# Which projection runs beside which mixer: Hyena's beside HGRN2, Mamba's beside Hyena, attention's beside Mamba

## Chip, cores and metric

One core of a Trainium2 chip. The metric is the device time of one launch, in microseconds (us).

## What is computed

A bidirectional encoder of two layers over a sequence of 512 positions and 1024 channels, all in float32. Each layer projects the normalised input once, lets four mixers work on slices of the projection's columns, projects their results back, and adds a mixture of 16 experts in which each expert chooses its 64 positions:

```
for l in range(DEPTH):
    hn = rmsnorm(x, norm_mix_w[l])
    pa, pb, pc, pd = jnp.split(hn @ w_in[l], splits, axis=-1)
    ya = hyena_mixer(pa, ...)                 # short conv, long conv by FFT, gate
    yb = mamba2_mixer(pb, ...)                # conv of 5 taps, silu, two scans, gate, rmsnorm
    yc = dilated_attention_mixer(pc, rel_bias)
    yd = hgrn2_mixer(pd, ...)                 # gated linear attention, two directions
    x = x + jnp.concatenate([ya, yb, yc, yd], axis=-1) @ w_out[l]
    x = x + expert_choice_moe(rmsnorm(x, norm_ffn_w[l]), router_w[l], ...)
return rmsnorm(x, final_norm_w)
```

The mixers do not depend on one another; only their sum does on all four. Each can thus run at any time once its own slice of the projection is there.

## The kernel before

One program computes everything; activations stay on the chip, weights are streamed in. The code is written as Python generators (`encoder`): each mixer and each projection is a stream that emits some instructions and then yields the weight of what it emitted. `weave` (L428) takes turns between two streams, always the one whose sum of yielded weights, divided by the number given with it, is least, until both are done; `chain` puts streams one after the other. The text order that comes out is the priority; a scheduler then places each engine's instructions in a fixed order, and `slots_in_order` (L157) holds tiles that share the same slots to the order of the text. The rings of slots that matter here are `bank_a`, three PSUM banks for `pcm`, `ptm` and `po`; `S`, three split weights; `W`, two raw weights; and `G`, nine pages for small temporaries.

A layer's mixers are written in four stages (L1590 to L1597). In each, one mixer (`hgrn`, `mamba`, `hyena`, `attn`), whose steps are short and hang on one another, is woven with work that does not depend on it: the projections of a later mixer and parts of the output projection.

The projections do their matmuls in three parts each, on weights and activations split into a high and a low part. `proj_cm` (L395 to L397) gives channels on partitions: 24 matmuls on one PSUM bank (`pcm`). `proj_tm` (L417 to L419) gives positions on partitions: 24 matmuls (`ptm`) for each of four blocks of 128 positions. The weight is split by GpSimd and VectorE (L380, L381), or by ScalarE and VectorE (L377, L378). `mamba_proj` (L685) computes four channel blocks with `proj_cm`, runs conv taps on each (L712 and L713 on VectorE) and a silu of three ScalarE activations (`me`, L446 to L448) and a multiplication (L449), and then one `proj_tm`. `hyena_proj` (L562 on) has six channel blocks, with two taps on each (L577, L578) and no silu. `attn_proj` (L917 on) has queries and keys by `proj_cm` (`aqs`, `aks`) and values by `proj_tm`.

Of the mixers, these lines matter. In `hgrn`, for each of two directions, the keys are transposed and copied by ScalarE (`gkT`, L1137), multiplied into states (`gU`, L1143), scanned on VectorE, the scores `gsc` (L1165) masked into `gP` (L1170, L1171), and both summed into `go` (L1177, L1186). At the end `go` is squared on ScalarE (`gsq`, L1195), normalised and gated on VectorE (`gy`, L1201 to L1203) and transposed by TensorE (`gyT`, L1208). `mamba` ends with `mo` (L860), its sums, gate and norm on VectorE and ScalarE, and the transposes `myT` (L893). `hyena` goes through transforms `hU` (L624), products with the filter's spectrum on VectorE (L629 to L658, the last of them `hz`), and the inverse transform `hy` (L668). `out_proj(l, [3])` adds HGRN2's part of the output projection (`po`, L1228 to L1230; 48 matmuls), and so needs `gyT`.

Behind the mixers come router and experts. Their weights are loaded ahead on SyncE's queue (`pieces`, the `we` loads of L1402), wherever a buffer is free; `atab` (L964), attention's four tables of position biases, are loaded there too, into buffers that the normalised input (`hT`) leaves.

Of the kernel before, what the change touches and what calls it, by code (L numbers as in the profile page):

```python
# [10 lines left out]
F32 = mybir.dt.float32  # L11
# [88 lines left out]
HW, HY = 28, 6  # L100
# [10 lines left out]
def encoder(ctx: ExitStack, tc: tile.TileContext, d, out, dbg=None, stages=None, nlayers=NL):  # L111
# [82 lines left out]
    def show(name, ap):  # L194
        if dbg and name in dbg:
            SY.dma_start(dbg[name], ap)
# [19 lines left out]
    def xrow(t):  # L216
        return X[t]
# [210 lines left out]
    def weave(*streams):  # L428

        at = [0.0] * len(streams)  # L430
        live = set(range(len(streams)))
        while live:
            i = min(live, key=lambda j: at[j] / streams[j][0])
            w = next(streams[i][1], None)
            if w is None:
                live.discard(i)
            else:
                at[i] += w

    def chain(*gens):  # L440
        for g in gens:
            yield from g
# [8 lines left out]
    MIX = {}  # L451
# [129 lines left out]
    def hyena_proj(l, hT, cols, st):  # L581
        raw1 = w_raw(l, HY0 + 256, 256)
        raw2 = w_raw(l, HY0 + 512, 256)
        uT = tl("N", [4, 256], "uT")

        def turn(c, a):
            ps = bank_a("uTp")
            for t in range(4):
                T.transpose(ps[:, t * P:(t + 1) * P], a[:, t::4], ident)
            A.activation(uT[:, :, c * P:(c + 1) * P], ps.rearrange("p (t c) -> p t c", t=4), AF.Copy)  # L590

        m = []
        for c in range(2):
            a = hyena_conv(hT, raw1, c * P, 2 + c, cols, tl("E", [L], "hu"))
            yield 5.1
            b = hyena_conv(hT, raw2, c * P, 4 + c, cols, tl("E", [L], "hu"))
            m.append(page([L], "hm"))
            V.tensor_mul(m[c], a, b)
            yield 5.1
        raw0 = w_raw(l, HY0, 256)  # L600
        x0 = tl("N", [2, L], "hx0")
        for c in range(2):
            hyena_conv(hT, raw0, c * P, c, cols, x0[:, c])
            turn(c, m[c])
            yield 6.0
        st[:] = uT, x0
# [78 lines left out]
    def mamba_proj(l, hT, cols, st):  # L685
        zt = tl("N", [4, 256], "mz")
        pack = tl("B", [576], "mpack")
        wdt = pack[:, 0:64].rearrange("p (k c) -> p k c", k=8)
        SY.dma_start(wdt, d["w_in"][l][:, MD0:MD0 + 8].rearrange("(k p) c -> p k c", p=P))

        def use(t, ps):
            V.tensor_scalar_max(zt[:, t], ps[:, :256], FLOOR)
            V.tensor_copy(pack[:, 64 + 8 * t:72 + 8 * t], ps[:, 256:264])

        xbc = []
        for ct in (2, 3, 0, 1):
            if ct % 2 == 0:
                raw = w_raw(l, MX0 + ct * P, 256)
                ub = tl("N", [2, L], "mu")
            ps = proj_cm(hT, raw, (ct % 2) * P)  # L700
            u = ub[:, ct % 2]

            def w(k):
                i = R_MCW + k * 4 + ct
                return cols[:, i:i + 1]

            A.activation(u, ps, AF.Identity, scale=w(2), bias=cols[:, R_MCB + ct:R_MCB + ct + 1])
            for k in (0, 1, 3, 4):
                s = k - 2
                o = slice(max(0, -s), L - max(0, s))  # L710
                i = slice(max(0, s), L - max(0, -s))
                V.scalar_tensor_tensor(u[:, o], ps[:, i], w(k), u[:, o], op0=ALU.mult, op1=ALU.add)  # L712
            V.tensor_scalar_max(u, u, FLOOR)  # L713
            e = tl("E", [L], "me")
            silu_inplace(u, e, u)
            xbc.append(u)
            yield 5.1
        yield from proj_tm(l, hT, [(MZ0, 256), (MD0, 8)], use, raws=[w_raw(l, MZ0, 256), wdt])
        st[:] = zt, pack, xbc
# [194 lines left out]
    def attn_proj(l, hT, st):  # L914


        half = (slice(0, 64), slice(64, 128))  # L917
        raw = w_raw(l, AQ0, 256)
        QS = []
        for i in range(2):  # L920
            ps = proj_cm(hT, raw, i * P, AM[0])
            qs = tl("N", [2, L], "aqs", F32R)
            for h in range(2):
                a, b = half[h], half[1 - h]
                A.activation(qs[a, h], ps[a], AF.Copy, scale=0.125)
                V.scalar_tensor_tensor(qs[b, h], ps[a], 0.125, qs[a, h].bitcast(F32),  # L926
                                       op0=ALU.mult, op1=ALU.subtract)
            QS.append(qs)
            yield 5.1
        raw = w_raw(l, AQ0 + 256, 256)  # L930
        KS = []
        for i in range(2):
            ps = proj_cm(hT, raw, i * P, AM[1])
            kh, kl = (tl("N", [2, L], "aks", F32R) for _ in range(2))
            for h in range(2):
                a, b = half[h], half[1 - h]
                A.activation(kh[a, h], ps[a], AF.Copy)
                V.tensor_sub(kl[a, h], ps[a], kh[a, h].bitcast(F32))
                if AM[2]:
                    A.activation(kh[b, h], kh[a, h].bitcast(F32), AF.Copy)  # L940
                    A.activation(kl[b, h], kl[a, h].bitcast(F32), AF.Copy)
                else:
                    G.tensor_copy(kh[b, h], kh[a, h])
                    G.tensor_copy(kl[b, h], kl[a, h])
            KS.append((kh, kl))
            yield 5.1
        v = tl("N", [4, 256], "av")

        def use(t, ps):
            A.activation(v[:, t], ps[:, :256], AF.Copy)  # L950

        yield from proj_tm(l, hT, [(AQ0 + 512, 256)], use, AM[3])
        st[:] = QS, KS, v
# [280 lines left out]
    def out_proj(l, ms):  # L1234
        raws = {m: out_raw(l, m) for m in ms}
        for n in range(2):
            W = {m: out_halves(raws[m], n) for m in ms}
            for t in range(4):
                out_part(t, n, [(m, k) for m in ms for k in range(2)], W)
                yield 1.28 * len(ms)  # L1240
# [318 lines left out]
    cols = [None] * NL  # L1559
    mbc = [None] * NL  # L1560
    fc = [None] * NL
    rows = iter(())
    spec = {}
    act_set(LNEXP)
    for l in range(nlayers):
        hT = norm_T(l, rows)
        s_h, s_m, s_y, s_a = [], [], [], []
        if l == 0:
            masks()
            proj = hgrn_proj(l, hT, s_h)  # L1570
            next(proj)
            inputs = filter_inputs()
            cols[0] = param_columns(0)
            for _ in range(FW[0]):
                next(proj)
            filt = filter_hidden(cols[0], spec, *inputs)
            next(filt)
            cols[1] = param_columns(1)
            hm = page([2, P], "hm", I32)
            SY.dma_start(hm, d["c_hmask"])  # L1580
            G.tensor_scalar(hmask, hm, 1, None, op0=ALU.mult)
            lb = lower_bounds(cols[1])
            scr = attn_table()
            for m in range(NL):
                mbc[m] = mamba_consts(m)
                fc[m] = ffn_consts(m)
            weave((FW[2] + 12, filt), (50, proj))
        else:
            run(hgrn_proj(l, hT, s_h))
        weave((40, hgrn(l, s_h, cols[l], lb)), (31, mamba_proj(l, hT, cols[l], s_m)))  # L1590
        show(f"mix3_{l}", MIX[3][0].bitcast(F32))
        weave((35, mamba(l, s_m, mbc[l], cols[l])), (32, hyena_proj(l, hT, cols[l], s_y)))
        show(f"mix1_{l}", MIX[1][0].bitcast(F32))
        weave((HW, hyena(l, s_y, spec)), (41, chain(out_proj(l, [3]), attn_proj(l, hT, s_a))))
        show(f"mix0_{l}", MIX[0][0].bitcast(F32))
        W = {}
        weave((40, attn(l, s_a, scr)), (25, chain(out_proj(l, [1, 0]), out_last(l, 2, W))))  # L1597
        show(f"mix2_{l}", MIX[2][0].bitcast(F32))
        view = {}
        load_next = pieces(l, view)  # L1600
        ring[:] = FIRST + ["H"] * 7 + EARLY
        while ring:
            next(load_next)
        st = []
        xd = dp.tile([2 * L, L], F32, name=f"xd{l}")
        route = router(fc[l][1], st, xd)
        for t in range(4):
            for n in range(2):
                out_part(t, n, [(2, 1)], W[n])
            next(route)  # L1610
        run(route)
        for t in range(4):
            show(f"xm{l}_{t}", xrow(t))
        if "moe" in stages:
            ra, = st
            rows = moe(l, ra, fc[l][0], load_next, view, xd, filter_again(spec) if l + 1 < nlayers else None)
# [32 lines left out]
```

## Time and profile before

| | us |
|---|---|
| median of 3 runs (1626.92 to 1629.75) | 1627.19 |
| the profiled execution | 1630.68 |
| its span | 1628.9 |
| TensorE busy (matmuls) in it | 1499.7 (92%) |
| VectorE | 789.8 (48%) |
| ScalarE | 394.0 (24%) |
| GpSimd | 212.2 (13%) |

The mean granted TensorE clock is 0.976 of full speed. The core moves 468.62 MB by DMA, most of it expert weights. In layer 0 the four mixer stages run from about 94 to 164 (HGRN2), 164 to 229 (Mamba), 229 to 276 (Hyena) and from 276 on (attention); experts start about 366. Layer 1 does the same some 795 us later. PE is TensorE's matmul, PEld its weight load, DVE VectorE, ACT ScalarE, POOL GpSimd, SP SyncE. In a timeline a row is one instruction or several alike, with the idle time before it and what released it in brackets; the name before the arrow is the tile written, those after it the tiles read.

### The profile page before, as it was taken

The numbers are of one execution on the slowest core, as the hardware profiler recorded it, in microseconds if no ns is written. First come the engines' busy times: TensorE is split into PE (matmuls) and PEld (weight loads), VectorE is DVE, ScalarE is ACT, GpSimd is POOL, SyncE is SP. The second block draws the span as 40 slices with busy tenths as digits, with TensorE's granted clock in tenths as the row PEclk, the third lists the DMA queues.
The fourth block names the chain that finished last, engine by engine and source line by source line (L and its number), as shares of the span: only waits on it lengthen the run. The fifth ranks groups of instructions, "written<-read, shape, count | busy, mean of one in ns | idle before, by whom it ended". The sixth has DMA issues, their size and how long they took to land.

```text
span 1628.9 us, 23876 instructions
## 1 busy us (share of the span) xinstructions
PE 1499.7 (92%) x9475; PEld 854.3 (52%) x9475; DVE 789.8 (48%) x1715; ACT 394.0 (24%) x805; POOL 212.2 (13%) x202
## 2 busy tenths in 40 slices
PE   7988999989999997989879899999899999998986
PEld 6677788753433442334368777787334433332332
DVE  6777777562333331432245777856523433332323
ACT  5244424430000000001162444343210101000012
POOL 3233232000000000000032323300000000000001
PEclk9999999989999999999999999999899999999999
DMA  5410225679999999999933211277799999999996
GB/s 172 128 53 28 79 78 185 228 266 367 421 419 421 421 419 400 421 420 419 421 115 104 79 53 53 78 282 267 251 420 421 418 421 421 421 420 420 420 420 255
DMA packets 153778, 468.62 MB, mean 288 GB/s; under 512 B 20440, under 2 KB 56696, under 8 KB 144962
## 3 DMA queue, kind: packets, MB, share of 16 engines
q1 hardware_dynamic: 145030, 455.10, 71.2%
q0 software_dynamic: 2240, 7.34, 1.1%
q10 hardware_dynamic: 6396, 4.65, 0.9%
q8 instruction: 75, 1.23, 0.3%
q14 instruction: 37, 0.30, 0.1%
HBM read 460.60 MB, written 6.44 MB: 287 GB/s over the span
## 4 chain that ended last, share of the span: by engine, by line
PE 59%; DMA 23%; DVE 8%; issue 4%; ACT 3%; POOL 2%; ACTq 0%; SPq 0%; DVEq 0%; POOLq 0%
PE eg L1410 10%; DMA we<-in_moe_w_down_dram 9%; PE ey L1410 8%; PE eu L1410 8%; DMA we<-in_moe_w_up_dram 8%; DMA we<-in_moe_w_gate_dram 5%; PE pcm L397 3%; PE pcm L395 3%; PE pcm L396 3%; PE ec L1481 2%; PE po L1228 2%; PE po L1229 2%; PE po L1230 2%; PE apv L992 1%; PE ptm L418 1%
## 5 line engine op out<-in xcount | busy, mean ns | idle before, releaser
L1410 PE MATMUL eu<-we,exT 128*64 128x512 f32 x1024 | 236.4, 598 | 16.5 <-DMA we<-in_moe_w_up_dram 14.4
L1410 PE MATMUL ey<-we,ehT 128*64 128x512 f32 x1024 | 233.7, 603 | 18.7 <-ACT ehT L1446 11.2
L1410 PE MATMUL eg<-we,exT 128*64 128x512 f32 x1024 | 229.9, 597 | 10.4 <-DMA we<-in_moe_w_gate_dram 6.2
L1410 PEld LDWEIGHTS eu<-we,exT 128*64 128x64 f32 x1024 | 68.4, 137 | 178.8 <-issue 94.4
L1309 DVE SCALAR_TENSOR_TENSOR ra<-er,ra,tie 128x512 bf16<-128x512 f32 x128 | 95.9, 749 | 127.5 <-PE er L1317 124.6
L1410 PEld LDWEIGHTS ey<-we,ehT 128*64 128x64 f32 x1024 | 71.2, 138 | 156.3 <-issue 106.1
L1410 PEld LDWEIGHTS eg<-we,exT 128*64 128x64 f32 x1024 | 69.3, 137 | 149.4 <-issue 112.0
L1463 DVE SCALAR_TENSOR_TENSOR eY<-ey,erg,eY 64x512 fp32r<-64x512 f32 x64 | 48.0, 749 | 191.2 <-ACT eY L1462 191.2
L1431 ACT ACTIVATE eh<-eg 128x512 f32<-128x512 f32 x32 | 19.1, 598 | 496.6 <-PE eg L1410 496.6
L397 PE MATMUL pcm<-hT,whl 128*128 128x512 f32 x320 | 129.3, 404 | 3.5 <-DVE whl L381 3.5
L1354 POOL DMA_INDIRECT exe<-xd,erow x28 | 27.8, 994 | 790.3 <-DVE erg L1335 663.0
L1482 DVE TENSOR_TENSOR x<-x,ec 128x512 f32<-128x512 f32 x128 | 81.0, 691 | 102.7 <-PE ec L1481 102.7
L395 PE MATMUL pcm<-hT,whl 128*128 128x512 f32 x320 | 129.6, 405 | 0.0
L396 PE MATMUL pcm<-hT,whl 128*128 128x512 f32 x320 | 129.4, 404 | 0.0
L1462 ACT ACTIVATE eY<-ey,erg 64x512 fp32r<-64x512 f32 x64 | 43.6, 682 | 269.9 <-PE ey L1410 245.5
L1438 DVE TENSOR_TENSOR eh<-eh,eu 128x512 f32<-128x512 f32 x32 | 22.0, 688 | 151.8 <-PE eu L1410 151.8
L417 PE MATMUL ptm<-wtm,hT 128*128 128x256 f32 (+1 forms) x256 | 76.0, 298 | 1.9 <-DVE aqs L926 1.7
L1481 PE MATMUL ec<-eY,eot 128*128 128x512 f32 x256 | 67.4, 405 | 10.2 <-DVE erow L1352 6.4
L418 PE MATMUL ptm<-wtm,hT 128*128 128x256 f32 (+1 forms) x256 | 74.7, 293 | 1.9 <-DVE wtm L381 1.9
L380 POOL TENSOR_SCALAR whl<-wraw 128x1024 fp32r<-128x1024 f32 x40 | 48.8, 1220 | 195.1 <-PE pcm L397 95.3
L419 PE MATMUL ptm<-wtm,hT 128*128 128x256 f32 (+1 forms) x256 | 73.5, 291 | 0.0
L397 PEld LDWEIGHTS pcm<-hT,whl 128*128 128x128 f32 x320 | 62.2, 194 | 19.0 <-DVE whl L381 3.9
(394 smaller groups left out, 2298.4 us busy)
## 6 DMA issues: line engine op xcount, KB each, us to landing
we<-in_moe_w_gate_dram SPq DMA_DIRECT2D x218, 512.0 KB
we<-in_moe_w_up_dram SPq DMA_DIRECT2D x208, 512.0 KB
we<-in_moe_w_down_dram SPq DMA_DIRECT2D x206, 512.0 KB
wraw<-in_w_in_dram SPq DMA_DIRECT2D x27, 1024.0 KB
we<-in_moe_w_down_dram SPq DMA_DIRECT2D x25, 1024.0 KB
we<-in_moe_w_up_dram SPq DMA_DIRECT2D x24, 1024.0 KB
we<-in_moe_w_gate_dram SPq DMA_DIRECT2D x19, 1024.0 KB
wo<-in_w_out_dram SPq DMA_DIRECT2D x8, 1024.0 KB
```

The source lines that it names most:

```text
L380: G.tensor_scalar(dst_hi, raw, 1.0, 0.0, op0=ALU.mult, op1=ALU.add)
L395: T.matmul(ps, w[:, 0, k, :], H[k], start=(k == 0), stop=False)
L396: T.matmul(ps, w[:, 0, k, :], Lo[k], start=False, stop=False)
L397: T.matmul(ps, w[:, 1, k, :], H[k], start=False, stop=(k == 7))
L417: T.matmul(dst, h, w[:, 0, k % 4], start=(k == 0), stop=False)
L418: T.matmul(dst, h, w[:, 1, k % 4], start=False, stop=False)
L419: T.matmul(dst, g, w[:, 0, k % 4], start=False, stop=(k == 7))
L1309: V.scalar_tensor_tensor(g, pr, ra[:, c, e, 0:1], tie[:, 384 - c * P:896 - c * P], op0=ALU.subtract, op1=ALU.is_gt, accum_out=k)
L1410: T.matmul(ps[f][64 * f:64 * f + 64], xT[:, j, h], qs[4 * h + j][:, f * 512:(f + 1) * 512], start=(h == 0 and j == 0), stop=(h == 1 and j ...
L1463: V.scalar_tensor_tensor(lo, src, w[c, 0:1], hi.bitcast(F32), op0=ALU.mult, op1=ALU.subtract)
L1481: T.matmul(ps, ot[:, t * P:(t + 1) * P], Y[i][q][n], start=(q == 0), stop=(q == 1))
L1482: V.tensor_add(xrow(t)[:, c], xrow(t)[:, c], ps)
```

## The change

Which projection is woven with which mixer. HGRN2's stage gets `hyena_proj` in place of `mamba_proj`; the second stage becomes Hyena's, beside `out_proj(l, [3])` and `mamba_proj`; the third becomes Mamba's, beside `attn_proj`. So Hyena runs ahead of Mamba. The fourth stage (attention) is as it was. The edit stands in the loop over layers, so it holds for both.

```diff
-        weave((40, hgrn(l, s_h, cols[l], lb)), (31, mamba_proj(l, hT, cols[l], s_m)))
+        weave((40, hgrn(l, s_h, cols[l], lb)), (32, hyena_proj(l, hT, cols[l], s_y)))
         show(f"mix3_{l}", MIX[3][0].bitcast(F32))
-        weave((35, mamba(l, s_m, mbc[l], cols[l])), (32, hyena_proj(l, hT, cols[l], s_y)))
+        weave((HW, hyena(l, s_y, spec)), (41, chain(out_proj(l, [3]), mamba_proj(l, hT, cols[l], s_m))))
+        show(f"mix0_{l}", MIX[0][0].bitcast(F32))
+        weave((35, mamba(l, s_m, mbc[l], cols[l])), (31, attn_proj(l, hT, s_a)))
         show(f"mix1_{l}", MIX[1][0].bitcast(F32))
-        weave((HW, hyena(l, s_y, spec)), (41, chain(out_proj(l, [3]), attn_proj(l, hT, s_a))))
-        show(f"mix0_{l}", MIX[0][0].bitcast(F32))
         W = {}
         weave((40, attn(l, s_a, scr)), (25, chain(out_proj(l, [1, 0]), out_last(l, 2, W))))
```

What it moves on TensorE's queue is shown at three places of layer 0. First the end of HGRN2, before. `pcm_1800` and `pcm_1871` are channel blocks of `hyena_proj`, the rows ahead of these are the last `go` and 21 more matmuls of `pcm_1800`:

```order
L395 MATMUL pcm_1800<-hT_124,whl_1797 128x512
L396 MATMUL pcm_1800<-hT_128,whl_1797 128x512
L397 MATMUL pcm_1800<-hT_124,whl_1797 128x512
L395 MATMUL pcm_1871<-hT_121,whl_1868 128x512
L1208 MATMUL gyT_1763<-pk,gy_1741 128x128 x4
L1208 MATMUL gyT_1770<-pk,gy_1741 128x128 x4
L748 MATMUL mcum_1828<-mpack_910,pk 128x4x4 x2
L749 MATMUL mcum_1828<-mpack_910,ones 128x32
```

And with the change, from the last `go` on; `po` is `out_proj(l, [3])`:

```order
L1186 MATMUL go_947<-gR_1401,gqi_1320 32x64
L1186 MATMUL go_947<-gR_1402,gqi_1320 32x64
L1186 MATMUL go_947<-gR_1401,gqi_1320 32x64
L1208 MATMUL gyT_1692<-pk,gy_1670 128x128 x4
L1208 MATMUL gyT_1699<-pk,gy_1670 128x128 x4
L1228 MATMUL po_1729<-wos_1726,mxh_1690 128x512
L1229 MATMUL po_1729<-wos_1726,mxh_1690 128x512
```

The 25 matmuls of `hyena_proj` that stood between `go` and `gyT` are no longer there: `gyT` follows the last `go`, and the output projection follows `gyT`.

Second, the middle of HGRN2: the last scores and the first products `go` of the second direction. Before, with `ptm_1590` and `ptm_1663` of `mamba_proj`:

```order
L419 MATMUL ptm_1663<-wtm_1391,hT_125 128x264
L417 MATMUL ptm_1663<-wtm_1391,hT_122 128x264
L418 MATMUL ptm_1663<-wtm_1391,hT_122 128x264
L1177 MATMUL go_954<-gv_260,gP_1585 32x64 x4
L1177 MATMUL go_955<-gv_260,gP_1585 32x64 x4
```

And with the change, where `uTp_1567` is four transposes of `hyena_proj`'s product:

```order
L1165 MATMUL gsc_1466<-gqk_1318,gqk_1319 32x32
L1165 MATMUL gsc_1465<-gqk_1318,gqk_1319 32x32
L1165 MATMUL gsc_1466<-gqk_1318,gqk_1319 32x32
L589 MATMUL uTp_1567<-pk,hm_1294 128x128 x4
L1177 MATMUL go_946<-gv_260,gP_1531 32x64 x4
L1177 MATMUL go_947<-gv_260,gP_1531 32x64 x4
```

The 22 `ptm` matmuls between the last `gsc` and the first `go` are gone; one group of transposes is there in their place.

Third, the end of Mamba. Before, with `po` of `out_proj(l, [3])`, 44 of which stand between the last `mo` and `myT`:

```order
L1228 MATMUL po_2401<-wos_2382,mxh_1761 128x512
L1229 MATMUL po_2401<-wos_2382,mxh_1761 128x512
L1230 MATMUL po_2401<-wos_2382,mxl_1762 128x512
L1228 MATMUL po_2420<-wos_2382,mxh_1761 128x512
L893 MATMUL myT_2303<-pk,my_1977 128x128
L893 MATMUL myT_2310<-pk,my_1977 128x128
```

And with the change; `ptm_2660` is the last block of `attn_proj`, and `alog` is attention's first product:

```order
L418 MATMUL ptm_2660<-wtm_2512,hT_124 128x256
L419 MATMUL ptm_2660<-wtm_2512,hT_128 128x256
L854 MATMUL my_2686<-mxt_2225,mw_2596 128x64 x4
L860 MATMUL mo_2691<-mprev_2278,mu_1822 128x256
L860 MATMUL mo_2692<-mprev_2278,mu_1822 128x256
L893 MATMUL myT_2728<-pk,my_2362 128x128 x4
L893 MATMUL myT_2735<-pk,my_2362 128x128 x4
L969 MATMUL alog_2749<-aks_2339,aqs_2201 128x512
L969 MATMUL alog_2749<-aks_2340,aqs_2201 128x512
L1228 MATMUL po_2767<-wos_2761,mxh_2726 128x512
```

`myT` follows `mo` directly, and attention and the rest of the output projection stand behind it.

## Rows read from the trace of the kernel before

**Rows 1.** the page's slices: DMA share in 40 equal slices of the span, in tenths

```profile
DMA  5410225679999999999933211277799999999996
```

**Rows 2.** chain of waits in the expert stages, by window: start us, us, what

```profile
567.51 12.85 DMA we<-in_moe_w_down_dram
...
1596.28 12.33 DMA we<-in_moe_w_down_dram
```

**Rows 3.** windows ahead of layer 0's experts: us, PE, PEld, DVE, ACT, POOL, PEclk, DMA share, GB/s

```profile
360.00:370.00 10.00, 9.08 (x54) 3.59 (x54) 5.38 (x19) 1.88 (x2) 0.00 (x0) 0.92 0.22 68
370.00:380.00 10.00, 10.00 (x64) 3.67 (x62) 3.00 (x10) 1.19 (x2) 0.00 (x0) 1.00 0.97 363
```

**Rows 4.** windows over three mixer stages of layer 0, same columns

```profile
94.00:164.00 70.00, 57.30 (x967) 47.60 (x966) 55.38 (x82) 34.17 (x54) 24.96 (x20) 0.90 0.16 47
164.00:229.00 65.00, 63.48 (x376) 50.19 (x375) 49.47 (x110) 27.34 (x74) 18.79 (x17) 1.00 0.25 75
229.00:276.00 47.00, 44.38 (x245) 38.79 (x244) 34.30 (x50) 16.04 (x27) 13.91 (x10) 0.93 0.37 128
```

**Rows 5.** waits of TensorE in layer 0, 86 to 276: total us, times, longest

```profile
PE gU L1143 <- ACT gkT L1137: 9.4, 2, 6.2
PE go L1177 <- DVE gP L1171: 2.3, 1, 2.3
PE pcm L397 <- DVE whl L381: 1.7, 1, 1.7
PE gyT L1208 <- DVE gy L1203: 0.7, 1, 0.7
```

**Rows 6.** waits of TensorE in layer 1, 895 to 1071

```profile
PE go L1177 <- DVE gP L1171: 3.1, 2, 2.2
PE ptm L418 <- DVE wtm L381: 1.6, 2, 1.0
PE gU L1143 <- ACT gkT L1137: 1.1, 2, 0.8
PE gyT L1208 <- DVE gy L1203: 0.8, 1, 0.8
```

**Rows 7.** timeline of TensorE in HGRN2's stage, both layers: start, us, operation, [idle before <-releaser]

```profile
116.85 1.98 PE L1143 MATMUL gU<-gve,gkT 64*64 64x128 f32 x32 [6.23 <-ACT gkT L1137]
...
149.20 1.33 PE L1143 MATMUL gU<-gve,gkT 64*64 64x128 f32 x32 [3.15 <-ACT gkT L1137]
...
157.52 0.43 PE L1177 MATMUL go<-gv,gP 32*32 32x64 f32 x16
...
951.70 0.44 PE L1177 MATMUL go<-gv,gP 32*32 32x64 f32 x16 [0.92 <-DVE gP L1171]
```

**Rows 8.** timeline of TensorE and ScalarE, end of HGRN2, layer 0

```profile
163.66 0.50 PE L395 MATMUL pcm<-hT,whl 128*128 128x512 f32 x1
...
170.37 1.06 PE L1208 MATMUL gyT<-pk,gy 128*128 128x128 f32 x8 [0.74 <-DVE gy L1203]
...
163.74 1.09 ACT L1195 ACTIVATE gsq<-go 128x512 f32<-128x512 f32 x2 [7.32 <-PE go L1186]
```

**Rows 9.** timeline of TensorE, end of Mamba, layer 0

```profile
218.03 0.70 PE L860 MATMUL mo<-mprev,mu 64*128 64x256 f32 x2
...
227.66 1.13 PE L893 MATMUL myT<-pk,my 128*128 128x128 f32 x8
```

**Rows 10.** windows of 4 us, columns as in rows 3

```profile
116.00:120.00 4.00, 3.15 (x154) 2.82 (x158) 3.81 (x4) 2.95 (x6) 0.00 (x0) 0.50 0.02 4
...
252.00:256.00 4.00, 2.79 (x7) 2.24 (x8) 3.94 (x7) 1.85 (x3) 3.90 (x2) 0.54 0.43 118
```

**Rows 11.** VectorE's groups by form, 94 to 276: count, busy us, mean ns, idle before

```profile
L381 DVE TENSOR_TENSOR whl<-wraw,whl 128x1024 fp32r<-128x1024 f32 x13 | 17.5, 1343 | 5.7 <-POOL whl L380 5.7
L712 DVE SCALAR_TENSOR_TENSOR mu<-pcm,cols,mu 128x510 f32<-128x510 f32 x8 | 5.9, 741 | 0.0
```

**Rows 12.** window at the start of attention, layer 0, columns as in rows 3

```profile
276.00:290.00 14.00, 14.00 (x77) 11.04 (x77) 8.12 (x22) 5.87 (x15) 0.00 (x0) 1.00 0.95 358
```

## The prediction

> **What bounds the kernel.** I read the views in this order: slices of the page, chain of waits, windows, TensorE's waits, timeline. In the slices the DMA row is at 9 from slice 9 to 20 and again from 27 on: the second half of each expert stage waits for expert weights, as the chain shows (a 12.85 us DMA in layer 0, a 12.33 us one 30 us before the end) [rows 1, 2]. Could a longer mixer part hide there? Only if the prefetch kept running meanwhile. From 360 to 370 us, just before the experts start, DMA share is 0.22, from 370 on 0.97 [rows 3]: all prefetch buffers are full by then, so time lost in the mixers is passed on to the end one for one. In the mixer stages that the change touches TensorE is busy 57 of 70, 63.5 of 65 and 44 of 47 us, and VectorE 55, 49 and 34 [rows 4]: TensorE sets their length, by its work plus its waits. That work stays the same, so I count TensorE's waits, before and after. Before, they are 9.4 us for gkT, 2.3 for gP, 1.7 for a weight split and 0.7 for gyT in layer 0 [rows 5], and 3.1, 1.1, 1.6 and 0.8 of the same kinds in layer 1 [rows 6].
>
> **The change part by part.** No instruction's shape changes; three projections trade mixers. What changes is what stands on TensorE's queue between a mixer's last product and the transposes of its result, and what shares VectorE with it.
>
> *End of HGRN2.* From the end of go to gyT (square, sum, root, two multiplications, gate) took 6.6 us: the square starts at 163.74, gyT at 170.37 [rows 8]. Twenty-five pcm matmuls of the next stage stood between, 0.23 us apart (163.66 to 169.5), and only 0.74 us of waiting was left. Now gyT follows go directly, and the work behind it (out_proj 3) needs gyT. With 0.9 us taken off for VectorE work of other streams that stood in between, the wait is 5.7: **+5.0 in each layer**. Bounds: 0 (gyT reached with cover) and +5.9.
>
> *Middle of HGRN2, second direction.* From the start of gU to the first go it took 8.3 us in layer 0 (149.20 to 157.52), 8.1 in layer 1 (ending with a 0.92 us wait) [rows 7]. TensorE's own part is gU and gsc, some 2.8 us; 22 ptm matmuls filled the rest. Now only one transpose of four is left there (0.4 us), so 5.0 to 5.4 us are bare: **+5.0 in layer 0, +4.5 in layer 1**. Bounds: 0 and +5.6.
>
> *First direction of HGRN2.* Here the change gives something. In layer 0 gU waited 6.23 us for gkT [rows 7], a ScalarE copy that stood behind the silu of mamba_proj, itself waiting for VectorE's conv taps. hyena_proj has no silu. I take layer 1's values (0.8 for gkT, 2.2 for gP, 1.8 between issues) as what is left: 5 against 9.0: **-4.0 in layer 0, 0 in layer 1** (4.8 already). Bounds: -9 and 0. The start of the second direction I leave at layer 0's 3.7 us in both layers, since its page is now held by hyena_proj's products until their transposes: 0 and **+2.3**.
>
> *Hyena's stage.* TensorE reaches hy after 48 po and 96 pcm matmuls, 144 x 0.23 = 33, and 3.5 us of transforms: 36 us. VectorE reaches hz, which hy needs, after hyena's own 30 instructions (0.68 us, so 20), 16 taps at 0.74 [rows 11] = 12, three clamps and products (2.5), three splits of 1.3 [rows 11] and eight residual additions (5.6): 44 us. The wait is thus up to 8.4; some of VectorE's rows follow hy's need, so I take 7, bounds 0 and 8.4. The waits before in this place (1.7 for the split and 0.9 for aqs; 3.3 in layer 1) are replaced: **+4.4 and +3.7**.
>
> *End of Mamba.* From mo to myT it took 8.9 us (218.73 to 227.66), with 44 po matmuls in between and no wait [rows 9]. Now myT follows mo directly, and nothing but attention, which comes behind it in the queue, could fill. A weight split of about 1.2 us that stood in VectorE's queue is no longer there: **+7.8 per layer**. Bounds: 0 and 8.9.
>
> *Hand-overs.* The po matmuls wait for the split of gyT and later of myT, and mamba's first chunk for its states: three at 0.75 (the 1.6 us for two in layer 1 [rows 6]): **+2.2 per layer**.
>
> *Clock.* After waits of 3 and 6 us the granted clock stood at 0.50 (the 1.2 GHz level) for some 6.5 us; 116 to 120 and, after two waits of 2.6 us in sum, 252 to 256 show it [rows 10]. Such a phase costs 3.2 us where TensorE is the bound. I expect one behind hy and one behind myT in each layer, 12.8, against before's three phases in layer 0 and one and a half in layer 1 where it was, some 10: **+3**. Bounds 0 and +13 (one more behind each bare wait).
>
> Sum: layer 0: 5.0 + 5.0 - 4.0 + 0 + 4.4 + 7.8 + 2.2 = 20.4; layer 1: 5.0 + 4.5 + 0 + 2.3 + 3.7 + 7.8 + 2.2 = 25.5; clock 3. Together **+49**. The profiled execution took 1630.7, 3.5 over the median of 1627.2; with it 1680, as a median **1676 us**.
>
> **The rivals.**
>
> *Only occupancy counts (1643).* The scheduler may find enough for TensorE at each bare place, and engines then count by load. VectorE in hyena's stage has mamba_proj (16 taps, 8 more of like length, 6 splits: 27), hyena (the 20 and some 4 for its end) and out_proj 3 (8 x 0.7 + 3 x 1.3 = 9.5), 60 us; TensorE has mamba_proj (96 pcm at 0.23 and 96 ptm at 0.12, 33.4), 48 po (10.9) and hyena's transforms (7.7), 52. VectorE becomes the bound, 8 us in each layer: 1627 + 16 = 1643. For it: waits of before were mostly at VectorE's and ScalarE's results [rows 5]. Against it: the order of TensorE's queue is fixed, and shows no cover. The Trainium skill ("Perfetto Trace Analysis", section "Optimization Strategy") says that regimes whose most-contended engines differ may gain by being interleaved; by that rule this pairing is a poor one, since the tap-heavy projection goes to the mixer that itself is heavy on VectorE; the loads above agree, and by it alone the time would be the 1643 just worked out. Chance 0.20.
>
> *Faster (1604).* The silu of mamba_proj on ScalarE's queue is what made HGRN2 late. If the move takes all of it away, the waits for gkT and gP go: 9.4 + 2.3 and 1.1 + 3.1 [rows 5, 6], 15.9 us, and with them two phases at the lower clock in layer 0's first stage, 2 x 3.2: 1627 - 23 = 1604. It decides if gyT and myT wait under 1 us each as now. For it: the 6.23 us row. Against it: layer 1 has the same silu and waits 0.8 there, and gyT and myT have lost what stood before them. Chance 0.06.
>
> *Late tables (1684).* attn_proj now ends last, so hT's buffers come free late, and attention's tables stand on SP's queue behind seven expert loads of 0.5 MB and one of 1 MB. With the two tables needed first (0.9 MB) that is 5.4 MB; at 358 GB/s [rows 12] it lands 15.1 us after the last projection, while apT needs it at some 17.8 (mamba's last products, the 7.8 us, po). Below 300 GB/s it is late; at 250 by 4 us in each layer: 1684. [...] Chance 0.10.
>
> *No change (1627).* The order of instructions could be what it was; the rows of the order speak against it. Chance 0.02.
>
> **How the numbers follow.** The sum has 0.60; 0.02 is for what I have not thought of. A difference of 0.2% (3.3 us) is about what a measurement of this kernel can tell. Faster by more: 0.06; within: 0.03; slower: 0.91. The range goes from 1642, which takes in the occupancy case, to 1696: 1676 with the clock's upper bound (+10), late tables (+8) and some of the open ends. The sum's own range is 1660 to 1690.
>
> **What would show it.** In the changed profile: TensorE's wait for gyT about 5.7 us (not 0.7), for myT about 8, for the first go of the second direction about 5, and about 7 for hy; the silu's 6.2 us wait for gkT gone; granted clock near 0.5 behind hy and myT. The expert stages should start some 20 to 25 us later than the same stage before, and last as long as they did. I am wrong if gyT or myT wait less than 2 us (their cover was not lost), if DMA share is high in the 10 us before the experts start, so that the delay is taken up, or if atab ends attention's first wait.

## The result, and the profile after

The changed kernel takes **1674.45 us** (1671.43 to 1678.11, 4 runs) against 1627.7 us (1626.92 to 1629.75, 4 runs): ratio 1.0276, 95% interval 1.0257 to 1.0296. It is slower by 46.8 us between medians. The profiled execution is the lowest of the four, with a span of 1669.7 us against 1628.9, 40.8 us more. The prediction was 1676, in a range of 1642 to 1696.

TensorE's waits in the mixer stages, which the prediction counted, are these. The changed kernel, layer 0, 86 to 310 us (who waits, for whom: total us, times, longest):

```profile
PE myT L893 <- DVE my L888: 8.7, 1, 8.7
PE go L1177 <- DVE gP L1171: 7.9, 2, 4.2
PE gyT L1208 <- DVE gy L1203: 6.0, 1, 6.0
PE ptm L417 <- DVE mu L712: 3.6, 1, 3.6
PE hy L668 <- DVE hz L635: 1.9, 1, 1.9
PE gU L1143 <- ACT gkT L1137: 1.8, 2, 1.0
PE pcm L397 <- DVE whl L381: 1.1, 1, 1.1
```

And layer 1, 895 to 1120:

```profile
PE myT L893 <- DVE my L888: 8.7, 1, 8.7
PE go L1177 <- DVE gP L1171: 7.1, 2, 3.9
PE gyT L1208 <- DVE gy L1203: 6.0, 1, 6.0
PE gU L1143 <- ACT gkT L1137: 4.5, 3, 2.5
PE ptm L417 <- DVE mu L712: 3.6, 1, 3.6
PE gkT L1135 <- ACT gqk L1112: 3.2, 1, 3.2
PE hy L668 <- DVE hz L635: 2.9, 1, 2.9
```

Against [rows 5] and [rows 6]: gyT waits 6.0 us in place of 0.7 and 0.8; myT 8.7, where nothing waited; in Hyena's stage pcm, ptm and hy wait 6.7 and 7.8 us together, where it had 2.6 and 3.3. The 9.4 us for gkT in layer 0 are down to 1.8, but in layer 1 they grew from 1.1 to 4.5, with 3.2 for gqk beside them. The timeline of TensorE in the changed kernel shows where the long ones are:

```profile
149.01 0.65 PE L1177 MATMUL go<-gv,gP 32*32 32x64 f32 x16 [4.20 <-DVE gP L1171]
...
159.76 1.94 PE L1208 MATMUL gyT<-pk,gy 128*128 128x128 f32 x8 [5.97 <-DVE gy L1203]
...
285.04 2.02 PE L893 MATMUL myT<-pk,my 128*128 128x128 f32 x8 [8.70 <-DVE my L888]
...
963.98 1.34 PE L1143 MATMUL gU<-gve,gkT 64*64 64x128 f32 x20 [2.54 <-ACT gkT L1137]
```

The second go of HGRN2 starts after 4.20 us of waiting, gyT after 5.97, myT after 8.70; the last row is the new wait of layer 1.

Does all of it reach the end? The timeline of TensorE shows the start of layer 0's experts, of layer 1 and of layer 1's experts. Before:

```profile
365.52 1.94 PE L1410 MATMUL eg<-we,exT 128*64 128x512 f32 x8 [0.22 <-DVE exT L1365]
...
835.70 1.54 PE L355 MATMUL xT<-pk,xn 128*128 128x128 f32 x6 [7.94 <-POOL xn L344]
...
1160.57 1.94 PE L1410 MATMUL eg<-we,exT 128*64 128x512 f32 x8 [0.22 <-DVE exT L1365]
```

And with the change:

```profile
376.40 1.94 PE L1410 MATMUL eg<-we,exT 128*64 128x512 f32 x8 [0.22 <-DVE exT L1365]
...
845.01 2.25 PE L355 MATMUL xT<-pk,xn 128*128 128x128 f32 x9 [8.08 <-POOL xn L344]
...
1201.01 2.37 PE L1410 MATMUL eg<-we,exT 128*64 128x512 f32 x10 [0.22 <-DVE exT L1365]
```

Experts and the norm behind them take 470.2 us before and 468.6 after (365.52 to 835.70, 376.40 to 845.01), the last part 468.3 and 468.7 (to the ends of the spans). So 9.3 of the 10.9 us that layer 0 was late came through, and all of layer 1's; the 1.6 us between are scatter, since this stretch took 468.6 to 471.1 us in the fourteen profiled executions of this study. DMA share in the 10 us before the experts is 0.36 in layer 0, where it was 0.29, and 0.27 in layer 1, as before: the delay was not taken up by prefetch. The window of the changed kernel in layer 0, columns as in [rows 3]:

```profile
366.40:376.40 10.00, 7.79 (x41) 2.74 (x41) 7.33 (x24) 1.88 (x2) 0.00 (x0) 0.76 0.36 146
```

Layer 1 from its start to its experts went from 324.9 to 356.0 us, +31.1. Layer 0 up to its experts shows +10.9 only, of which an earlier piece has to be set apart: filter and first projections, ahead of the first changed stage. The last transform of the filter (`fk`, L560) starts at 88.08 before and at 82.97 after. That piece moves from one profiled execution to the next: in those of this study `fk` starts between 83.0 and 86.1 us where the granted clock is full ahead of it, and between 88.1 and 92.4 where a phase at the 1.2 GHz level falls there (68 to 75 us in the one of before). From `fk` to the experts, layer 0 lost 16.0 us. The account of the two spans is thus -5.1 + 16.0 - 1.6 + 31.1 + 0.4 = 40.8, and without the filter's piece 45.9, near the 46.8 between the medians.

### The profile page after: what moved, and what is told of

The parts are those of the page before. It is cut to its first block, busy times and chain, and to the rows that moved or that the text cites. A ratio compares the mean times of both kernels' runs of the same rounds, so it can differ in the third digit from the quotient of the medians.

```text
span 1669.7 us, 23886 instructions
## 1 busy us (share of the span) xinstructions
PE 1497.9 (90%) x9475; PEld 859.0 (51%) x9475; DVE 796.4 (48%) x1715; ACT 395.2 (24%) x805; POOL 207.6 (12%) x202
## 4 chain that ended last, share of the span: by engine, by line
PE 52%; DMA 24%; DVE 12%; issue 6%; ACT 4%; POOL 2%; ACTq 0%; SPq 0%; DVEq 0%; POOLq 0%
DMA we<-in_moe_w_down_dram 9%; PE eg L1410 9%; PE eu L1410 8%; PE ey L1410 8%; DMA we<-in_moe_w_up_dram 7%; DMA we<-in_moe_w_gate_dram 6%; PE ec L1481 2%; PE pcm L395 2%; PE pcm L397 2%; PE pcm L396 2%; PE po L1228 2%; PE po L1229 1%; PE po L1230 1%; PE apv L992 1%; PE ptm L418 1%
## 5 line engine op out<-in xcount | busy, mean ns | idle before, releaser
L1410 PE MATMUL ey<-we,ehT 128*64 128x512 f32 x1024 | 233.4, 602 | 19.4 <-ACT ehT L1446 11.2
L397 PE MATMUL pcm<-hT,whl 128*128 128x512 f32 x320 | 125.5, 392 | 2.3 <-DVE whl L381 2.3
L395 PE MATMUL pcm<-hT,whl 128*128 128x512 f32 x320 | 126.8, 396 | 0.0
L396 PE MATMUL pcm<-hT,whl 128*128 128x512 f32 x320 | 125.4, 392 | 0.0
```

What stands on the lines that cost most here:

```text
L395: T.matmul(ps, w[:, 0, k, :], H[k], start=(k == 0), stop=False)
L396: T.matmul(ps, w[:, 0, k, :], Lo[k], start=False, stop=False)
L397: T.matmul(ps, w[:, 1, k, :], H[k], start=False, stop=(k == 7))
L1410: T.matmul(ps[f][64 * f:64 * f + 64], xT[:, j, h], qs[4 * h + j][:, f * 512:(f + 1) * 512], start=(h == 0 and j == 0), stop=(h == 1 and j ...
```

## The experiments

Theory: three places of TensorE's queue lost the work that stood in them (second go, gyT, myT), and Hyena's stage waits for VectorE. Rivals: only the loads of the stages count; TensorE's work sets the stages and the waits are no price; a moved silu is what matters. The kernel before, run beside them, had medians of 1630.16 us (beside the runs with mamba_proj first, out_proj last, 60 matmuls and two taps), 1628.28 (30 matmuls, weight 20, all covers, attention's projection) and 1629.71 (the three with splits moved and the one without the silu); distances to the changed kernel are of medians, and by the ratios they come out within 3 us the same.

**Cover for gyT.** mamba_proj is written ahead of out_proj(l, [3]).

```diff
-        weave((HW, hyena(l, s_y, spec)), (41, chain(out_proj(l, [3]), mamba_proj(l, hT, cols[l], s_m))))
+        weave((HW, hyena(l, s_y, spec)), (41, chain(mamba_proj(l, hT, cols[l], s_m), out_proj(l, [3]))))
```

> The changed kernel with mamba_proj written ahead of out_proj(l, [3]) in Hyena's stage, so that 23 pcm matmuls (5.2 us) stand between the last go and gyT again; loads of the stages stay the same. Lost cover: gyT waits under 1 us instead of 6.0 in both layers, the waits around hy stay (6 to 8 us), and the time falls by some 10 us, to about 1664. Only occupancy counts: the stage's VectorE load is unchanged, the wait moves to hy, and the time stays at 1674.

Measured: 1664.98 us (1661.84 to 1668.61), ratio 1.0211, interval 1.0185 to 1.0236: 9.5 us below the changed kernel. Its waits in layer 0 (86 to 310):

```profile
PE ptm L417 <- DVE mu L712: 8.8, 2, 5.9
PE go L1177 <- DVE gP L1171: 5.2, 2, 3.7
PE ptm L418 <- DVE wtm L381: 2.4, 1, 2.4
PE gyT L1208 <- DVE gy L1203: 0.5, 1, 0.5
```

gyT waits 0.5 us, with the same work to do. The occupancy rival said 1674 and is out as the whole story. But the edit did more than cover gyT. In its timeline eleven pcm stand ahead of the second go too, whose wait falls from 4.20 and 3.88 us to 1.51 in both layers, and ten ahead of layer 1's gU, whose 2.54 us are gone. The waits in Hyena's stage were expected to stay and grew instead, from 6.7 to 11.2 us in layer 0 and from 7.8 to 10.9 in layer 1 (8.8 us now for conv taps at the ptm, none at hy). So the 9.5 us are a balance of several shifts and not the price of gyT's cover alone.

**Cover for myT as well.** out_proj(l, [3]) goes from Hyena's stage to the end of Mamba's.

```diff
-        weave((HW, hyena(l, s_y, spec)), (41, chain(out_proj(l, [3]), mamba_proj(l, hT, cols[l], s_m))))
+        weave((HW, hyena(l, s_y, spec)), (41, mamba_proj(l, hT, cols[l], s_m)))
...
-        weave((35, mamba(l, s_m, mbc[l], cols[l])), (31, attn_proj(l, hT, s_a)))
+        weave((35, mamba(l, s_m, mbc[l], cols[l])), (31, chain(attn_proj(l, hT, s_a), out_proj(l, [3]))))
```

> The changed kernel with out_proj(l, [3]) moved out of Hyena's stage to the end of Mamba's, behind attn_proj: its po matmuls then stand between the last mo and myT, and pcm matmuls between go and gyT. Lost cover: gyT under 1 us (from 6.0) and myT under 1 us (from 8.7) in both layers, 5 + 8.7 each, some 4 us of lower clock behind myT back, and 2 to 3 us per layer given back at hy, which TensorE reaches 11 us earlier and VectorE 9: about 1648. Only occupancy counts: VectorE 9 us over TensorE in Hyena's stage as now: 1670 to 1675.

Measured: 1642.21 us (1638.49 to 1645.66), ratio 1.0079, interval 1.005 to 1.0108: 32 us below the changed kernel and 6 below what was expected. Its waits of TensorE in layer 0 (86 to 310):

```profile
PE myT L893 <- DVE my L888: 0.5, 1, 0.5
PE gyT L1208 <- DVE gy L1203: 0.5, 1, 0.5
```

Both transposes wait 0.5 us. As in the run before, the second go (1.5 us) and layer 1's gU got cover as well, which was not expected, and Hyena's stage waits longer, 11.4 and 9.1 us. Over both layers TensorE's listed waits fall by 29 us, close to the 32 of the medians. About seven tenths of the loss hung on where 48 po matmuls and the first pcm stand.

**Work put into the wait for myT.** 60 matmuls that nothing reads, between the last mo and myT.

```diff
+        fill = bank_a("fill")
+        for _ in range(60):
+            T.matmul(fill[:, :P], ident, ident, start=True, stop=True)
         mix_tile(1)
```

> The changed kernel with 60 matmuls of 128x128 that nothing reads between mamba's last mo and myT, about 8 us of TensorE work per layer. Lost cover: the wait for myT is bare, the added work fits into it and the time does not rise (-3 to +2 us); if the lower clock behind myT comes from that wait, it goes, worth up to 1.4 to 2.1 us per layer: 1671 to 1676. If TensorE's work were what sets the stage: +16, 1690.

Measured: 1686.29 us (1683.27 to 1691.56), ratio 1.0359, interval 1.0331 to 1.0386: 12 us above the changed kernel, a miss. Its timeline of TensorE says why (start, us, operation; no bracket, no wait):

```profile
279.49 13.66 PE L891 MATMUL fill<-pk 128*128 128x128 f32 x120
292.99 1.04 PE L896 MATMUL myT<-pk,my 128*128 128x128 f32 x8
```

Sixty took 13.66 us, not 8: the trace has 120 records, two for each 128x128 float32 matmul, 0.114 us each. They outlasted the wait of 8.7 by 5 us in each layer, and myT waits for nothing. So the run was repeated with 30:

> As the filler before, with half of it: one 128x128 float32 matmul took 0.228 us there, not the 0.13 assumed, so that 60 took 13.7 us and outlasted the wait of 8.7; 30 take 6.8 and fit. Lost cover: myT starts where it does in the changed kernel, some 1.9 us of wait left; time 1671 to 1675 (the lower clock behind myT, 2.1 and 1.4 us, goes or stays). If TensorE's work set that stage: +13.6, 1688.

Measured: 1674.28 us (1673.1 to 1680.04), ratio 1.0291, interval 1.0261 to 1.032. With 6.8 us of TensorE work more in each layer the time is that of the changed kernel. Its timeline of TensorE:

```profile
288.07 0.41 PE L896 MATMUL myT<-pk,my 128*128 128x128 f32 x2 [1.78 <-DVE my L888]
```

The wait is bare: work fits into it at no cost. TensorE's work does not set this place. It also held the clock: in the changed kernel the granted clock is at the 1.2 GHz level from 279 to 290 us, around this wait; with the 30 matmuls it stays at full in both layers there. That is worth little: from `fk` to alog layer 0 takes 203.7 us in the changed kernel and 202.7 here, from its first row to alog layer 1 265.8 and 263.6, 1 to 2 us per layer, too little for the medians.

**Cover for the second go and gyT by one number.**

```diff
-        weave((40, hgrn(l, s_h, cols[l], lb)), (32, hyena_proj(l, hT, cols[l], s_y)))
+        weave((40, hgrn(l, s_h, cols[l], lb)), (20, hyena_proj(l, hT, cols[l], s_y)))
```

> The changed kernel with one number: hyena_proj has weight 20 in place of 32 beside HGRN2, so that it lags, and 19 of its pcm matmuls (4.3 us) fall between the last gsc and the first go of the second direction, 29 (6.6 us) between the last go and gyT. Nothing else is moved. Lost cover: gyT 6.0 to under 1, the second go 4.2 to under 1, in each layer: 1674 - 2 x (5.2 + 3.5) = 1657; 1652 to 1662. Only occupancy: the loads of the stages do not change, 1674.

Measured: 1650.7 us (1649.86 to 1656.51), ratio 1.0133, interval 1.011 to 1.0155: 24 us below the changed kernel, 7 more than the sum. Layer 1's waits (895 to 1130):

```profile
PE go L1177 <- DVE gP L1171: 3.9, 2, 2.1
PE gU L1143 <- ACT gkT L1137: 1.0, 1, 1.0
PE gkT L1135 <- ACT gqk L1112: 0.7, 1, 0.7
PE gyT L1208 <- DVE gy L1203: 0.2, 1, 0.2
```

gyT waits 0.2, in layer 0 not at all, while Hyena's stage waits as it did in the changed kernel (6.5 and 7.6 us) and myT its 8.7: here gyT's cover is seen without the shifts of the run with mamba_proj first. The surplus is layer 1's new wait, which went with it: gU and gkT waited 4.5 + 3.2 us in the changed kernel and 1.0 + 0.7 here. The go rows add up two directions; the longest is 2.1 us in layer 1 but 4.7 in layer 0, so there the cover went to the second direction and the first now waits more.

**All covers at once.** Weight 20, and out_proj(l, [3]) behind attn_proj, the two edits above together.

> Weight 20 for hyena_proj, and out_proj(l, [3]) behind attn_proj: covers for the second go, gyT and myT at once. Lost cover: against 1642 for the move of out_proj alone only the second go is new, 3 us per layer: 1636, 1632 to 1640; Hyena's stage keeps its waits for conv taps (11 us in layer 0), since VectorE has 53 us there against 41 of TensorE. Only occupancy: 1642.

Measured: 1637.38 us (1636.31 to 1640.17), ratio 1.0058, interval 1.004 to 1.0077. As expected within 2 us. It is still 9 us above the kernel before, and the longest waits of TensorE left in its layer 0 are in Hyena's stage and at go:

```profile
PE ptm L417 <- DVE mu L712: 7.3, 2, 6.1
PE go L1177 <- DVE gP L1171: 7.1, 2, 4.7
PE ptm L418 <- DVE wtm L381: 4.2, 1, 4.2
```

**Does VectorE's load set Hyena's stage?** Two runs took VectorE's work out of it. The first leaves out two of four shifted conv taps of mamba_proj:

```diff
-            for k in (0, 1, 3, 4):
+            for k in (1, 3):
```

> The changed kernel with two of the four shifted conv taps of mamba_proj left out (k = 0 and 4), eight VectorE instructions of 0.74 us per layer, 5.9 us, all in Hyena's stage. VectorE sets that stage: the waits at hy and the ptm before it (6.7 and 7.8 us) fall by about 5 us in each layer, time about 1664. If Hyena's own chain, or TensorE, sets it: 1673 to 1675.

Measured: 1674.4 us (1670.33 to 1676.37), ratio 1.0273, interval 1.0245 to 1.0301: no gain. Its wait of TensorE in Hyena's stage, layer 0:

```profile
PE ptm L417 <- DVE mu L712: 4.5, 1, 4.5
```

The wait at hy is gone, but the scheduler had put hz ahead of the third block's taps, and the ptm, which needs the PSUM bank that these taps read, waits 4.5 us for them; Mamba's first product waits 1.7 where it waited 0.2. From gyT to that product (mcum, L748) the changed kernel takes 71.5 us in layer 0 and 72.1 in layer 1, this one 69.4 and 68.3. The second keeps the taps and takes the weight splits of mamba_proj off VectorE (ScalarE copies, GpSimd subtracts):

```diff
-            ps = proj_cm(hT, raw, (ct % 2) * P)
+            ps = proj_cm(hT, raw, (ct % 2) * P, 1)
...
-        yield from proj_tm(l, hT, [(MZ0, 256), (MD0, 8)], use, raws=[w_raw(l, MZ0, 256), wdt])
+        yield from proj_tm(l, hT, [(MZ0, 256), (MD0, 8)], use, (1, 1), raws=[w_raw(l, MZ0, 256), wdt])
```

> The changed kernel with the weight splits of mamba_proj made by ScalarE (copy) and GpSimd (difference) in place of GpSimd and VectorE: some 7 us of VectorE's work per layer leave Hyena's stage, nothing else is moved by hand. VectorE sets that stage: the waits in it (1.1 + 3.6 + 1.9 us, and 1.1 + 3.6 + 3.1) fall by 5 us per layer, time about 1664. If the order of VectorE's queue alone sets them, as the two taps left out suggested (1674): 1672 to 1676. If GpSimd's differences are late, the pcm wait for whl instead: 1680 or more.

Measured: 1677.84 us (1671.28 to 1681.03), ratio 1.0282, interval 1.0247 to 1.0317: no gain either. The wait at the ptm is 4.8 us and mcum's 1.7, as without the taps; gyT to mcum takes 68.7 and 69.4 us. From `fk` to the end both take what the changed kernel takes, 1586.6 and 1586.8 us against 1586.7: other stretches (layer 0's experts, layer 1 up to gyT) were 4 us longer in these profiled executions, and why is not shown. So 6 to 7 us of VectorE work less shorten the stage by 2 to 4, and of these only 0.5 to 2 are waits; the rest is less busy time of TensorE, with less time at the 1.2 GHz level. Load is at most a part of what sets the stage. The order of VectorE's queue, which each edit changed, can be the rest; how much each has is left open.

**The same splits with all covers, and in the kernel before.**

> Both covers, weight 20, and mamba_proj's splits off VectorE. VectorE sets Hyena's stage: its waits there (7.3 + 4.2 us in layer 0) fall by 5 to 7 us per layer, 1637 - 12 = 1625, about the kernel before. If not: 1637. Late differences: 1645 or more.

Measured: 1639.95 us (1637.87 to 1645.7), ratio 1.0074, interval 1.0049 to 1.0099. Not the 1625 hoped for. In layer 0 the ptm's wait falls from 7.3 to 2.3 us and wtm's goes, but hy then waits 4.2 for hz.

> The kernel before with the same splits moved off VectorE, a control: there mamba_proj stands in HGRN2's stage, whose waits are for a chain and not for VectorE's load. Lost cover: gains 0 to 4 us in layer 0's first stage from earlier conv taps (1624 to 1630), or loses, since ScalarE's copies stand ahead of gkT: up to 1636. Occupancy: VectorE sets no stage there, 1628.

Measured: 1638.94 us (1637.38 to 1648.9), ratio 1.0079, interval 1.0046 to 1.0113. The move costs 9 us in the kernel before by the medians, 13 by the ratio: gU waits 10.7 us in layer 0 where it waited 9.4 [rows 5], and go 3.8 for GpSimd. From its list of waits, layer 0:

```profile
PE gU L1143 <- ACT gkT L1137: 10.7, 2, 8.9
PE go L1177 <- POOL wtm L378: 3.8, 1, 3.8
```

In the changed kernel with these splits GpSimd takes 2.4 to 2.7 us for a difference of 128x1024 that took VectorE 1.2 to 1.3 [rows 11].

**Attention's projection into Hyena's stage**, against the kernel with all covers.

```diff
-        weave((HW, hyena(l, s_y, spec)), (41, mamba_proj(l, hT, cols[l], s_m)))
+        ap = attn_proj(l, hT, s_a)
+        weave((HW, hyena(l, s_y, spec)), (41, chain(mamba_proj(l, hT, cols[l], s_m), (next(ap) for _ in range(2)))))
...
-        weave((35, mamba(l, s_m, mbc[l], cols[l])), (31, chain(attn_proj(l, hT, s_a), out_proj(l, [3]))))
+        weave((35, mamba(l, s_m, mbc[l], cols[l])), (22, chain(ap, out_proj(l, [3]))))
```

> As the one before, and the first two channel blocks of attn_proj (48 pcm, 10.9 us) moved from Mamba's stage into Hyena's behind mamba_proj, with weight 22 in place of 31 beside Mamba so that 36 po matmuls still stand before myT. If VectorE sets Hyena's stage, its waits are filled by up to 11 us per layer and Mamba's stage gets shorter: 1636 - 2 x 8 = 1620, 1612 to 1630, below both kernels. If conv taps bind by the PSUM banks alone (the pcm in the queue behind the taps wait as well), nothing is won: 1634 to 1640.

Measured: 1652.32 us (1647.45 to 1656.43), ratio 1.0142, interval 1.0109 to 1.0175, 15 us above the kernel with all covers: wrong way round. Layer 0 of its timeline:

```profile
194.93 0.56 PE L417 MATMUL ptm<-wtm,hT 128*128 128x264 f32 x1 [6.06 <-DVE mu L712]
...
232.37 0.52 PE L748 MATMUL mcum<-mpack,pk 128*128 128x16 f32 x4
...
285.65 1.14 PE L893 MATMUL myT<-pk,my 128*128 128x128 f32 x8 [0.42 <-DVE my L888]
```

The wait of 6.06 us, and one of 4.22 behind it, stand at mamba_proj's ptm, ahead of the added pcm in the queue, so these fill nothing: from gyT to mcum it takes 71.2 us in place of 60.3, the 10.9 us of the moved work in full. And Mamba's stage, from mcum to myT, took 53.3 us with that much less work, 56.8 before the move: Mamba's own chain needs about that long, and the work taken from beside it was cover.

**The silu alone.** The kernel before, with the silu of mamba_proj's conv channels left out.

```diff
-            e = tl("E", [L], "me")
-            silu_inplace(u, e, u)
```

> The kernel before without the silu of mamba_proj's conv channels (12 ScalarE activations and 4 VectorE products per layer, left out). It shows alone what HGRN2 gains when no silu stands ahead of its gkT copies. Lost cover: gU's wait of 6.2 us in layer 0 goes to 0.8 and the lower clock behind it too, layer 1 hardly moves, and gyT and myT wait as in the kernel before: -8 to -12, 1616 to 1620. If the silu sat beside other waits: within 3 us of 1628.

Measured: 1623.03 us (1619.74 to 1630.99, 10 runs), ratio 0.9971, interval 0.9949 to 0.9993: 5 to 7 us faster, less than the 8 to 12 expected. Its waits of TensorE in layer 0 (line numbers are two lower here):

```profile
PE go L1175 <- DVE gP L1169: 11.6, 2, 10.6
PE gU L1141 <- ACT gkT L1135: 1.7, 2, 0.9
```

gU's wait falls from 9.4 to 1.7, but the wait for gP, next on the same chain, grows from 2.3 [rows 5] to 11.6. The silu was in front of the wait and not the whole of it. TensorE's idle time from `fk` to alog did not fall at all (16.9 us before, 18.2 here); its busy time did, from 171.2 to 166.4 us for the same matmuls, as a phase at the 1.2 GHz level near 150 us is gone and much of the one near 116 falls into the long wait. So what the silu's absence gave in layer 0 is clock, not waiting.

No version here is below the kernel before with the whole computation in it. The nearest, 1637.38, has the changed pairing with all covers.

## Why the prediction was right

**The bound.** TensorE's work plus its waits set the mixer stages, and what is lost there reaches the end one for one. The expert stages took 470.2 and 468.6 us. Windows from `fk` and from layer 1's start to the experts, columns as in [rows 3], show what the stages lost. Before:

```profile
88.08:365.52 277.44, 255.36 (x2137) 203.43 (x2135) 197.68 (x410) 116.02 (x251) 58.45 (x47) 0.94 0.39 134
835.70:1160.57 324.87, 307.80 (x2464) 249.30 (x2464) 221.54 (x445) 140.47 (x302) 67.51 (x56) 0.96 0.37 128
```

And with the change:

```profile
82.97:376.40 293.43, 254.54 (x2137) 204.26 (x2135) 201.58 (x410) 116.85 (x251) 56.26 (x47) 0.92 0.37 127
845.01:1201.01 356.00, 311.62 (x2463) 253.82 (x2464) 226.24 (x445) 140.84 (x302) 63.68 (x56) 0.92 0.34 117
```

TensorE's time without work (length less busy time) grew by 16.8 us in layer 0 and 27.3 in layer 1, its busy time by 3.0 in all. The waits below add up to 16.7 and 27.2. So the bound is shown, and the account closes.

**End of HGRN2** (+5.0 per layer): 5.97 us of wait in both layers, +5.2. That it is the lost cover is shown by the runs that put matmuls there again: 0.5 us with mamba_proj first, 0 and 0.2 with weight 20, where Hyena's stage and myT kept their waits.

**End of Mamba** (+7.8): 8.70 us in both. Shown bare by 30 matmuls that cost nothing, and gone with po behind attn_proj.

**Middle of HGRN2** (+5.0 and +4.5): 4.2 us in layer 0, 3.9 against 0.9 in layer 1, so +4.2 and +3.0, a little less than worked out: gP was ready about 1 us earlier than the order of the rows let me expect.

**First direction** (-4.0 and 0): gU 0.8 and go 3.7 in layer 0, 4.5 against 9.0; 0.7 and 3.2 in layer 1 against 4.8. So -4.5 and -0.9. The row was right, but the reason only half: without the silu, in the kernel before, gP's wait took the place of gkT's. Here mamba_proj's conv taps left the stage too; that this is why gP did not wait longer is argued, not shown.

**Start of the second direction** (0 and +2.3): this was the term that was mis-sized in layer 1. Layer 0 had 2.2 us in place of 3.7; layer 1 7.6 in place of 1.4, +6.2. The chain is seen on ScalarE and VectorE of the changed kernel:

```profile
958.84 0.68 DVE L1108 TENSOR_TENSOR gl<-gl,ga 128x512 f32<-128x512 f32 x1
...
959.55 0.72 ACT L1112 ACTIVATE gqk<-gl,ln1m 128x512 f32<-128x512 f32 x1 [1.04 <-DVE gl L1108]
...
960.70 1.89 ACT L1148 ACTIVATE gU<-gU 128x512 f32<-128x512 f32 x2
...
963.35 0.58 ACT L1137 ACTIVATE gkT<-gkT 128x512 f32<-128x512 f32 x1
```

VectorE makes gl behind a tap of hyena_proj (958.18), ScalarE's gqk waits for it, and the next gkT copy stands behind two copies of gU. A tap stands ahead of gl in layer 0 as well (134.39), so it is not the difference. There the second gqk started 0.9 us after gU, here 3.6, and nine pcm stood between the second gkT and its gU (from 137.50 on), where layer 1 has none left after 954.23. With mamba_proj first, ten pcm stand between layer 1's last gkT and gU, and gU's 2.54 us are gone while gkT still waits 3.4 for gqk. So gU's part is lost cover once more; why gqk comes late in layer 1 is left open. I had named a page held too long: the place was right, but these waits end at ScalarE's copies. With hyena_proj at weight 20 they are 1.6 in place of 7.6 us.

**Hyena's stage** (+4.4 and +3.7, waits of 7): pcm, ptm and hy wait 6.7 and 7.8 us, +4.1 and +4.5. The size was right; that VectorE's load sets it is not shown. 6 to 7 us of work taken off VectorE took 0.5 to 2 us off these waits, and what was left settled on the next thing in VectorE's queue.

**Hand-overs** (+2.2): mrow, mcum and mcT have 1.1 us and the po after gyT and myT no wait in the list: about +0.5. Too large.

**Clock** (+3): windows of some microseconds in the changed kernel show 0.50 (1.2 GHz) beside the waits for hy and myT:

```profile
204.00:208.00 4.00, 2.45 (x9) 1.89 (x9) 3.90 (x8) 1.89 (x3) 0.00 (x0) 0.50 0.00 0
...
279.00:284.00 5.00, 0.00 (x0) 0.00 (x0) 1.87 (x4) 2.21 (x10) 0.82 (x2) 0.51 1.00 355
```

Much of a phase lies in the wait itself (279 to 284: no busy time at all), where it costs nothing. What reached the work is TensorE's busy time, +3.0 us for the same matmuls in the windows above: the value taken. Weighting each microsecond of these windows by TensorE's busy time and the granted clock would give 22.2 us lost before and 30.8 after, +8.6; the account above has no room for that much, so this weighting overrates it here. A phase stands at gyT's wait and at the second go's too, which I had not counted.

By layers, 22 and 27 us were expected, clock included, and 16.0 and 31.1 measured: the sum of 47.1 is close to 49 because misses of both signs cancel. That is luck to some degree; the three lost covers, some seven tenths of the sum, were each right within 2 us.

**The rivals.** Occupancy alone is refuted: the work was the same in the run with mamba_proj first and in the one with weight 20, 9.5 and 24 us apart from the changed kernel. (Its 27 us for mamba_proj on VectorE add up from their own terms to 25.6, which would make the case 1641.) What the Trainium skill says of interleaving regimes with different most-contended engines ("Perfetto Trace Analysis", section "Optimization Strategy") bears on Hyena's stage, where VectorE was busy without a gap from 175 to 205 us, but it names the smaller part of the loss, 4 us per layer at most. Faster by the silu: the first direction's gain is real, 4.5 us in layer 0, and a tenth of what was lost. Late tables: one sign of being wrong did appear. In layer 0 a table ends attention's first wait, on VectorE:

```profile
289.24 0.69 DVE L972 CUSTOM_DVE_ANT_0 alg<-alog,atab 128x512 f32<-128x512 f32 x1 [0.67 <-DMA atab<-scr]
```

Before, that row waited for no table. The price is 0.7 us at most: layer 1 has no such wait, no wait of TensorE names the tables, and from alog to the experts attention and router take 89.7 us where they took 89.5. The rival's sum lets the tables land behind all loads issued ahead of them; no run here shows whether they do. No change: the order of the rows held.

## What to carry to other kernels

In a stage that weaves a chain with independent work, look at the end of the chain: what stands in the queue between its last product and the transposes that hand it on must last as long as the vector work there (6 and 9 us here), and must not itself need the result. Moving 48 matmuls that were already there, or one weight of the interleave, was worth 10 to 30 us, while taking load off VectorE gained nothing. Before taking a busy engine's work away, see what it does next in order: several of these edits only moved the wait to the next thing in the same queue.

## What the runs showed of the hardware that was not expected

A 128x128 matmul of float32 operands has two records in the trace and took 0.228 us (60 in 13.66 us), against 0.13 for the transposes of the same size (eight gyT in 1.06 us [rows 8]). And a phase at the 1.2 GHz level falls into the filter's part, ahead of all that was changed, in 6 of 14 profiled executions (3.4 us of clock in that of before, none in that of the changed kernel), which is as large as some terms of the sum: one profiled pair alone would have shown 41 us where the medians show 47.
